# Latent attention on one Trainium2 core: scores with keys on partitions instead of queries, the row maximum folded into a matmul, and the division by the row sum moved behind the output matmul

## The chip, the core and the metric

The kernel runs on one core of a Trainium2 chip. TensorE (PE) multiplies matrices into PSUM; VectorE (DVE), ScalarE (ACT) and GpSimd (POOL) work on SBUF, the first two also on PSUM; SyncE (SP) issues the DMAs. The metric is the device time of one execution in microseconds. A few of the profile's names: PEld is the weight load of TensorE, PEclk the share of its full clock that was granted, and L123 is line 123 of the kernel.

## What is computed

Two layers run over 1024 latent tokens and 256 context tokens of width 1024. The first is a gated linear recurrence (HGRN2), the second multi-head latent attention. The change lies in the second layer alone, which is for 16 heads:

```python
def _attend(q_nope, q_pe, k_nope, k_pe, v):
    s = (jnp.einsum('bqhd,bkhd->bhqk', q_nope, k_nope, preferred_element_type=jnp.float32)
         + jnp.einsum('bqhr,bkr->bhqk', q_pe, k_pe, preferred_element_type=jnp.float32))
    p = jax.nn.softmax(s * MLA_SCALE, axis=-1)
    return jnp.einsum('bhqk,bkhd->bqhd', p.astype(v.dtype), v)
...
    def readout(o, z):
        B, L = o.shape[:2]
        return (o.reshape(B, L, D_INNER) * jax.nn.silu(z)) @ w_out
```

There are 1024 queries and 1280 keys a head. Keys and values of all heads come from one 128-wide latent and a 64-wide rotary part, so the kernel folds each head's key matrix into its queries and each head's value matrix into its output: all heads use the same `kh`, `kl`, `kr` and `vh`, `vl`.

## The kernel before

Everything is float32. To multiply at the rate of the faster float32r format without losing digits, a value is split into a rounded high part and a low part that holds the rest (`split`, L208: a ScalarE cast, then a VectorE subtraction), and a product is three matmuls: high by high, high by low, low by high (`mm3`, L263 to L265).

A tile is 128 tokens. Attention has 128 query tiles (8 for each of 16 heads), in 64 units of two. Per query tile `attn_scores` (L839) holds the queries still and streams the keys past them in blocks of 512, 512 and 256 columns, five matmuls a block (L855 to L859). A row of scores then lies in one partition: VectorE takes its extreme (L861, L867), ScalarE takes the exponential and the row sum (L871), VectorE divides the row by the sum (L877 to L882). Per unit `attn_values` (L885) transposes these probabilities on TensorE, 20 blocks of 128x128 (L902, tile `pt`), splits them (ScalarE `ph` L214, VectorE `pl` L215, both reading `pt` in PSUM), accumulates `pv` with 30 matmuls of 256 columns (L263 to L265), splits the result (`o32`, `oh` on ScalarE, `ol` on GpSimd, L920 to L922), multiplies by the head's value matrix (three matmuls), multiplies by the gate `za` on VectorE (L927, tile `ya`), and stores it to DRAM.

`attn_prep` (L783) makes the next head's operands in steps: two small float32 matmuls and the split of their result (`wqh`, `wql`), for every second head eight transposes of the rotary queries with their split (`qrh`, `qrl`, L818 to L826), and two blocks of 512 queries (six matmuls of 512 columns each, split into `wl`, `wh`). Each step goes through the PSUM tag `pt`, of which there are three buffers.

`attend` (L930) sorts all these steps by a time written out by hand. This order binds TensorE alone (`AT_ORDER`); a scheduler orders the other engines. Behind attention comes the output product of 16 heads; its first 8 heads for two token tiles (`lead`, L1197) are laid over the end of attention. SP's order is the scheduler's, before and after.

Of the kernel before, what the change touches and what calls it, by code (L numbers as in the profile page):

```python
# [9 lines left out]
F32 = mybir.dt.float32  # L10
# [27 lines left out]
class Net:  # L38
# [631 lines left out]
    def mla_in(self, pool, pp, kp, a, hh, hl, st):  # L670
# [6 lines left out]
        for c in range(NT):  # L677
# [39 lines left out]
            )  # L717
            if lat:
                j = c - NC
                nc.scalar.activation(junk, ps[:, 192:448], AF.Square, accum_out=ss[:, 1:2])  # L720
                r = self.rsq(pool, ss[:, 1:2], QR, 1)
                qn = t(pool, [P, QR], F32, "qn")
                nc.vector.tensor_scalar(qn, ps[:, 192:448], r, None, ALU.mult)
                q32 = t(pool, [P, 2, P], F32, "q32")
                for k in range(2):
                    nc.tensor.transpose(tp[:, (2 + k) * P : (3 + k) * P], qn[:, k * P : (k + 1) * P], self.ident)
                    nc.scalar.activation(q32[:, k], tp[:, (2 + k) * P : (3 + k) * P], AF.Copy, scale=qg[:, k : k + 1])
                js = slice(j * P, (j + 1) * P)
                self.split(st["qh"][:, :, js], st["ql"][:, :, js], q32)
# [53 lines left out]
    def attn_prep(self, pool, pp, a, st, qrD, zT, h, box):  # L783
# [23 lines left out]
        if h % 2 == 0:  # L807
# [6 lines left out]
            for b, n in self.qgs:  # L814
                sl = slice(b * P, (b + n) * P)
                ps = t(pp, [P, 512], F32, G_TAG)
                for j in range(n):
                    nc.tensor.transpose(ps[:, j * P : (j + 1) * P], qr[:, b + j], self.ident)  # L818
                for i, (rh, rl) in enumerate(box["pair"]):
                    own, twin = (slice(0, 64), slice(64, P))[:: 1 - 2 * i]  # L820
                    src = ps[own, : n * P]
                    nc.scalar.activation(rh[own, sl], src, AF.Copy, scale=SCALE)
# [16 lines left out]
    def attn_scores(self, pool, pp, st, box, i, prs):  # L839
        nc, t, NT = self.nc, self.t, self.NT  # L840
        mm = nc.tensor.matmul
        LK = NT * P
        blocks = [(o, min(512, LK - o)) for o in range(0, LK, 512)]
        nb = len(blocks)
        h, j = divmod(i, self.NL)
        qah, qal, rh, rl = box[h][:4]
        js = slice(j * P, (j + 1) * P)
        mx = t(pool, [P, 4], F32, "mx")
        sm = t(pool, [P, 4], F32, "sm")
        pr = t(pool, [P, LK], F32, "pr")  # L850
        sc = []
        for b, (o, w) in enumerate(blocks):
            s = t(pp, [P, 512], F32, "s")
            ks = slice(o, o + w)
            mm(s[:, :w], qah[:, js], st["kh"][:, ks], start=True, stop=False)  # L855
            mm(s[:, :w], qah[:, js], st["kl"][:, ks], start=False, stop=False)  # L856
            mm(s[:, :w], qal[:, js], st["kh"][:, ks], start=False, stop=False)  # L857
            mm(s[:, :w], rh[:, js], st["kr"][:, ks], start=False, stop=False)  # L858
            mm(s[:, :w], rl[:, js], st["kr"][:, ks], start=False, stop=True)  # L859
            with self.tc.high_priority(offset=AT_PRIO):  # L860
                nc.vector.tensor_reduce(mx[:, b : b + 1], s[:, :w], AX.X, ALU.min)  # L861
            sc.append(s)
            if b < nb - 1:
                yield
        nm = t(pool, [P, 1], F32, "nm")
        with self.tc.high_priority(offset=AT_PRIO):
            nc.vector.tensor_reduce(nm, mx[:, :nb], AX.X, ALU.min)  # L867
        for b, (o, w) in enumerate(blocks):
            yield
            with self.tc.high_priority(offset=EXP_PRIO):  # L870
                nc.scalar.activation(  # L871
                    pr[:, o : o + w], sc[b][:, :w], AF.Exp, bias=nm, scale=-1.0,
                    accum_out=sm[:, b : b + 1],
                )
        yield
        rs = t(pool, [P, 1], F32, "rs")
        nc.vector.tensor_reduce(rs, sm[:, :nb], AX.X, ALU.add)  # L877
        nc.vector.reciprocal(rs, rs)
        if i % NORM_ACT[1] < NORM_ACT[0]:
            nc.scalar.activation(pr, pr, AF.Copy, scale=rs)  # L880
        else:
            nc.vector.tensor_scalar(pr, pr, rs, None, ALU.mult)  # L882
        prs[i] = pr

    def attn_values(self, pool, pp, st, box, u, prs, yT):  # L885
        nc, t, NT = self.nc, self.t, self.NT
        tiles = [i for i in (2 * u, 2 * u + 1) if i < self.NH * self.NL]
        h, b = divmod(tiles[0], self.NL)
        n = len(tiles)
        N = n * P  # L890
        wvh, wvl, z = box[h][4:]
        np_ = -(-NT // 2)
        parts = {}
        acc = None
        for e in range(np_ + PV_LAG):
            if e < np_:
                m = min(2, NT - 2 * e)
                tp = t(pp, [P, 2, 2 * P], F32, "pt")
                for c in range(m):
                    for j, i in enumerate(tiles):  # L900
                        k = 2 * e + c
                        nc.tensor.transpose(  # L902
                            tp[:, c, j * P : (j + 1) * P], prs[i][:, k * P : (k + 1) * P], self.ident
                        )
                ph = t(pool, [P, 2, 2 * P], F32R, "ph")
                pl = t(pool, [P, 2, 2 * P], F32R, "pl")
                self.split(ph[:, :m, :N], pl[:, :m, :N], tp[:, :m, :N])
                parts[e] = (m, ph, pl)
            if e >= PV_LAG:
                if acc is None:  # L910
                    acc = self.pv[:, u % 2]
                m, ph, pl = parts.pop(e - PV_LAG)
                for c in range(m):
                    k = 2 * (e - PV_LAG) + c
                    self.mm3(acc[:, :N], st["vh"][:, k], st["vl"][:, k], ph[:, c, :N], pl[:, c, :N], k == 0, k == NT - 1)
            yield
        oh = t(pool, [P, 2 * P], F32R, "oh")
        ol = t(pool, [P, 2 * P], F32R, "ol")
        o32 = t(pool, [P, 2 * P], F32, "o32")
        nc.scalar.copy(o32[:, :N], acc[:, :N])  # L920
        nc.scalar.copy(oh[:, :N], o32[:, :N])
        nc.gpsimd.tensor_tensor(ol[:, :N], o32[:, :N], v32(oh[:, :N]), ALU.subtract)  # L922
        yield
        ps = t(pp, [P, 512], F32, G_TAG)
        self.mm3(ps[:, :N], wvh, wvl, oh[:, :N], ol[:, :N], True, True)
        y = t(pool, [P, 2 * P], F32, "ya")
        nc.vector.tensor_tensor(y[:, :N], ps[:, :N], z[:, b * P : b * P + N], ALU.mult)  # L927
        nc.sync.dma_start(yT[h][:, b * P : b * P + N], y[:, :N])

    def attend(self, pool, pp, a, st, qrD, zT, yT, box, tail):  # L930
        NL, NH = self.NL, self.NH
        n = NH * NL
        self.pv = self.t(pp, [P, 2, 2 * P], F32, "pv")
        prs = {}
        steps = []
        for h in range(1, NH):
            t0 = NL * (h - 1) + 3 + AT_LAG
            g = self.attn_prep(pool, pp, a, st, qrD, zT, h, box)
            gap = min(0.9, (NL - 4 - AT_LAG) / 5)
            steps += [(t0 + (e + (PREP_LATE if e > 1 and h % 2 == 0 else 0)) * gap, g) for e in range(6)]  # L940
        nb = -(-self.NT * P // 512)
        for i in range(n):
            g = self.attn_scores(pool, pp, st, box, i, prs)
            steps += [(i + b / nb, g) for b in range(nb)]
            steps += [(i + (nb - 1) / nb + EXP_AT[min(b, 2)], g) for b in range(nb)]
            steps += [(i + NORM_AT, g)]
        np_ = -(-self.NT // 2)
        for u in range(-(-n // 2)):
            g = self.attn_values(pool, pp, st, box, u, prs, yT)
            steps += [(2 * u + 2 + AT_LAG + e * 2 / np_, g) for e in range(np_ + PV_LAG + 2)]  # L950
        steps += [(n + TAIL_AT + TAIL_GAP * k, tail) for k in range(NH)]
        steps = sorted(enumerate(steps), key=lambda x: (x[1][0], x[0]))
        for _, (_, g) in steps:
            next(g, None)
# [24 lines left out]
def body(tc, a, out, dims):  # L979
    D, NH, NC, NL = dims  # L980
    NT = NC + NL
    with ExitStack() as ctx:
# [8 lines left out]
        zT = [t(dpool, [P, NL * P], F32, f"zT_{h}") for h in range(NH)]  # L991
        yT1 = [t(dpool, [P, NL * P], F32, f"yT1_{h}") for h in range(NH)]
# [113 lines left out]
        with ExitStack() as c3:  # L1106
# [55 lines left out]
            "kr": t(kpool, [P, NT * P], F32R, "kr"),  # L1162
            "qh": t(kpool, [P, 2, NL * P], F32R, "qh"),
            "ql": t(kpool, [P, 2, NL * P], F32R, "ql"),
        }
        with ExitStack() as c4:
# [30 lines left out]
        def lead():  # L1197
            head.extend(accs(sp, "s", 2))
            for k in range(K_LEAD if NH > K_LEAD else NH // 2):
                ld = net.op_load(mo, a["w_mo"], yT1, k, mg[0])  # L1200
# [4 lines left out]
        with ExitStack() as c5:  # L1205
            pool = Split(early, EARLY, Bufs(TP(c5, "at", 1), AT_BUFS))
            pp = Split(ep, EARLY, sp)
            with tc.manual_schedule(engines=AT_ORDER):
# [51 lines left out]
PREP_LATE = 0.5  # L1260
# [3 lines left out]
TAIL_AT = 0.2  # L1264
TAIL_GAP = 0.45
# [3 lines left out]
    "qr": 1, "wk": 2, "qrh0": 2, "qrl0": 2, "qrh1": 2, "qrl1": 2, "pr": 7, "ph": 4, "pl": 4,  # L1269
    "mx": 4, "sm": 4, "nm": 4, "rs": 4, "wvh": 2, "wvl": 2, "ya": 2, "oh": 2, "ol": 2,  # L1270
# [4 lines left out]
EARLY = {"wk", "qr", "za0", "wv32", "wvh", "wvl", "wqh", "wql", "qrh0", "qrl0", "pt", "pv"}  # L1275
AT_PSUM = {"s": 4, "pt": 3, "pv": 1}
G_TAG = "pt"
EXP_AT = (0.1, 0.25, 0.4)
NORM_ACT = (0, 2)
AT_PRIO = 60  # L1280
EXP_PRIO = 0
NORM_AT = 1.0
SCALE = -float((128 + ROPE) ** -0.5)
AT_ORDER = {mybir.EngineType.PE}
AT_LAG = 1.0
PV_LAG = 2
# [104 lines left out]
```

## Time and profile before

| | before |
|---|---|
| median of 3 runs | 3146.39 us (3146.16 to 3146.5) |
| the profiled execution's own time | 3146.84 us |
| its span, first to last instruction | 3145.1 us |
| mean granted TensorE clock | 0.995 |
| first and last score matmul | 2130.8 and 2949.2 us |
| last matmul into `pv` | 2983.0 us |
| busy in 2254 to 2306 us (one head) | PE 52.00, DVE 39.98, ACT 31.97, POOL 3.48 us |

The times in a timeline row are the start within the span and the duration, both in us. A matmul's duration holds its way through the array; the next one starts long before it ends, so the cost of a matmul in a stream is the distance between two starts. A group's row has busy time, then the mean duration in ns, then the idle time before it.

### The profile page before, as it was taken

Reading aid. Unit: us, or ns where it says so; the run is one execution under the profiler, and the core shown is the slowest. Engines: PE = TensorE matmul, PEld = TensorE weight load, DVE = VectorE, ACT = ScalarE, POOL = GpSimd, SP = SyncE. Lnnn points to the kernel's source line nnn. Section 1 sums busy time; section 2 is a strip of 40 time slices with the busy share of each in tenths; the row PEclk is TensorE's granted clock in tenths of the full one; section 3 lists DMA queues with packets and bytes.
Section 4 is the critical chain, followed back from the end, with each engine's and each line's share of the span. In section 5 each row is a group of like instructions: output and inputs, shape, how many; then the busy total and the mean of one; then the engine's idle time right before and its main releaser. Section 6 shows DMA issues by size and latency. Waiting matters only on the chain.

```text
span 3145.1 us, 51475 instructions
## 1 busy us (share of the span) xinstructions
PE 3108.3 (99%) x19412; PEld 2782.5 (88%) x19412; DVE 2164.4 (69%) x4898; ACT 1729.6 (55%) x4263; POOL 188.3 (6%) x305
## 2 busy tenths in 40 slices
PE   8899999999999999999999999999999999999999
PEld 7889989899898998988988888788999999999887
DVE  7777688776886758757585563536777777777642
ACT  6556465564655646655475563224666666666532
POOL 0000000000000000000000011000010000000000
PEclk8999999999999999999999999999999999999999
DMA  5110212102111021010127661430101011101261
GB/s 212 43 56 23 74 36 63 56 23 75 36 56 57 24 73 36 30 40 25 41 69 243 222 197 45 141 117 24 41 30 38 24 34 34 34 28 38 69 219 57
DMA packets 100009, 218.88 MB, mean 70 GB/s; under 512 B 10289, under 2 KB 47409, under 8 KB 99761
## 3 DMA queue, kind: packets, MB, share of 16 engines
q1 hardware_dynamic: 99760, 215.59, 21.1%
q8 instruction: 153, 2.51, 0.3%
q14 instruction: 96, 0.78, 0.1%
HBM read 175.70 MB, written 39.85 MB: 69 GB/s over the span
## 4 chain that ended last, share of the span: by engine, by line
PE 92%; DVE 3%; issue 2%; DMA 2%; ACT 1%; POOL 0%; SPq 0%; DVEq 0%; POOLq 0%; ACTq 0%
PE g L265 12%; PE g L264 12%; PE g L263 12%; PE lv L335 6%; PE pt L902 4%; PE o L486 3%; PE pv L263 2%; PE s L855 2%; PE pv L264 2%; PE pv L265 2%; PE s L856 2%; PE s L858 2%; PE s L859 2%; PE s L857 2%; PE lv L263 2%; PE lv L265 2%
## 5 line engine op out<-in xcount | busy, mean ns | idle before, releaser
L263 PE MATMUL g<-hh,wh 128*128 128x512 f32 (+1 forms) x1512 | 548.4, 363 | 3.3 <-DVE hh L253 1.6
L265 PE MATMUL g<-hl,wh 128*128 128x512 f32 (+1 forms) x1512 | 542.4, 360 | 3.0 <-DVE hl L254 3.0
L264 PE MATMUL g<-hh,wl 128*128 128x512 f32 (+1 forms) x1512 | 543.3, 359 | 0.0
L263 PEld LDWEIGHTS g<-hh,wh 128*128 128x128 f32 x1512 | 286.5, 189 | 40.6 <-DVE hh L253 2.0
L265 PEld LDWEIGHTS g<-hl,wh 128*128 128x128 f32 x1512 | 285.7, 189 | 39.0 <-DVE hl L254 3.8
L215 DVE TENSOR_TENSOR wl<-raw,wh 128x1024 fp32r<-128x1024 f32 (+1 forms) x170 | 207.7, 1224 | 160.8 <-ACT wh L214 149.4
L264 PEld LDWEIGHTS g<-hh,wl 128*128 128x128 f32 x1512 | 286.4, 189 | 35.9
L861 DVE TENSOR_REDUCE mx<-s 128x1 f32<-128x512 f32 (+1 forms) x384 | 229.7, 599 | 94.5 <-PE s L859 93.0
L871 ACT ACTIVATE pr<-s,nm 128x512 f32<-128x512 f32 (+1 forms) x384 | 232.7, 615 | 99.1 <-DVE nm L867 92.8
L335 PE MATMUL lv<-QX,KX 128*128 128x128 f32 x1920 | 263.1, 275 | 5.8 <-ACT QX L407 4.3
L335 PEld LDWEIGHTS lv<-QX,KX 128*128 128x128 f32 x1920 | 246.6, 192 | 14.8 <-ACT QX L407 5.5
L214 ACT CAST wh<-raw 128x1024 fp32r<-128x1024 f32 (+1 forms) x170 | 178.0, 1049 | 121.8 <-PE lv L264 38.2
L214 ACT CAST ph<-pt 128x512 fp32r<-128x512 f32 x320 | 187.8, 587 | 96.2 <-PE pt L902 86.6
L215 DVE TENSOR_TENSOR pl<-pt,ph 128x512 fp32r<-128x512 f32 x320 | 219.4, 686 | 12.6 <-ACT ph L214 12.5
L263 PE MATMUL g<-wh,hh 128*128 128x256 f32 (+2 forms) x676 | 197.6, 293 | 0.0
L263 PE MATMUL pv<-ph,vh 128*128 128x256 f32 x640 | 196.7, 307 | 0.0
L265 PE MATMUL g<-wl,hh 128*128 128x256 f32 (+2 forms) x676 | 196.4, 291 | 0.0
L902 PE MATMUL pt<-ident,pr 128*128 128x128 f32 x1280 | 192.5, 273 | 0.1
L264 PE MATMUL g<-wh,hl 128*128 128x256 f32 (+1 forms) x654 | 187.9, 287 | 0.0
L407 ACT COPY KX<-K 128x256 f32<-128x256 f32 (+1 forms) x288 | 109.6, 381 | 131.3 <-PE lv L335 71.3
L265 PE MATMUL pv<-pl,vh 128*128 128x256 f32 x640 | 180.2, 282 | 0.0
L264 PE MATMUL pv<-ph,vl 128*128 128x256 f32 x640 | 180.0, 281 | 0.0
(557 smaller groups left out, 7918.3 us busy)
## 6 DMA issues: line engine op xcount, KB each, us to landing
raw<-in_w_o SPq DMA_DIRECT2D x64, 512.0 KB, 3.8
raw<-in_w_qfbz SPq DMA_DIRECT2D x61, 512.0 KB, 3.8
raw<-in_ada_wT SPq DMA_DIRECT2D x32, 512.0 KB, 3.6
raw<-in_w_mo SPq DMA_DIRECT2D x24, 512.0 KB, 3.9
raw<-in_w_v SPq DMA_DIRECT2D x16, 512.0 KB, 3.6
yT<-Z SPq DMA_DIRECT2D x32, 256.0 KB, 2.0
raw<-in_w_z SPq DMA_DIRECT2D x16, 512.0 KB, 4.1
pyr<-yT SPq DMA_DIRECT2D x64, 128.0 KB, 3.7
```

The costliest lines, as they stand in the source:

```text
L214: nc.scalar.copy(hi, src)
L215: (eng or nc.vector).tensor_tensor(lo, src, v32(hi), ALU.subtract)
L263: mm(ps, lh, rh, start=first, stop=False)
L264: mm(ps, ll, rh, start=False, stop=False)
L265: mm(ps, lh, rl, start=False, stop=last)
L335: nc.tensor.matmul(ps[:, sl], lhs[:, sl], rhs[:, sl], start=True, stop=True)
L407: cp(m12(N[:]), m12(Y))
L486: nc.tensor.matmul(o[:, sl], l, r, start=i == 0, stop=i == len(ops) - 1)
L855: mm(s[:, :w], qah[:, js], st["kh"][:, ks], start=True, stop=False)
L861: nc.vector.tensor_reduce(mx[:, b : b + 1], s[:, :w], AX.X, ALU.min)
L871: nc.scalar.activation(pr[:, o : o + w], sc[b][:, :w], AF.Exp, bias=nm, scale=-1.0, accum_out=sm[:, b : b + 1],)
L902: nc.tensor.transpose(tp[:, c, j * P : (j + 1) * P], prs[i][:, k * P : (k + 1) * P], self.ident)
```

## The change

**Scores.** A unit of two query tiles now holds 128 keys still and streams 256 queries: ten key tiles, two to a PSUM bank, four matmuls each (L859), so that a column of `s` is a query and the probabilities come out with keys on partitions, as the second product wants them. The 20 transposes are gone.

**Maximum.** It must now be taken across partitions: VectorE takes it over the five banks elementwise (`m2`, L863 and L865) and over the last pair (`mf`, L873), TensorE transposes `mf` twice (L876), VectorE reduces (`mr`, L879), TensorE spreads the result over partitions (L882), ScalarE writes its negative into row 64 of the low rotary queries (L887). A fifth matmul of each key tile, `k5` by `rl` (L893), adds the low rotary part and the negative maximum to the scores still lying in PSUM; row 64 of `k5` is one. Only then comes the exponential (L896), without a bias and without the sum.

**Sum and division.** GpSimd adds the five probability tiles (four additions of 128x512, one of 128x256, L904 to L910). One unit after the values TensorE sums over partitions with a matmul by ones (L949), VectorE takes the reciprocal (L954), it goes to DRAM and comes back spread over partitions (L955, L960), and GpSimd multiplies `ya` by it (L962).

**Splits and buffers.** Probabilities are split out of SBUF, not PSUM. `ol` moves from GpSimd to VectorE (L945). PSUM has one buffer of `pt` instead of three; `mt` and `s5` take the other two.

**Order.** `attend` writes out one loop over units: scores of unit u, values of u-2, output of u-3, splits of u-1, a step of `attn_prep` behind the second and the fourth score bank. The order now binds TensorE, VectorE, ScalarE and GpSimd (`AT_HAND`). In the last five units `lead` also loads and splits the first four output weights.

```diff
+            nc.scalar.copy(st["k5"][:64, sl], tp[:64, P : 2 * P])
...
+                for i, (l, r) in enumerate(((kh, qah), (kl, qah), (kh, qal), (kr, rh))):
+                    mm(o, l[:, ks], r[:, js], start=c + i == 0, stop=c == m - 1 and i == 3)
...
+                    nc.vector.tensor_tensor(m2[:, :m], m2[:, :m], s[:, :m], ALU.max)
...
+            nc.tensor.transpose(mt[:, 0, j * P : (j + 1) * P], mf[:, j * P : (j + 1) * P], self.ident)
...
+            nc.vector.tensor_reduce(mr, mt[:, 0, :N].rearrange("p (j k) -> p j k", k=P), AX.X, ALU.max)
...
+            nc.scalar.activation(rl[64:65, js], mt[64:65, 1, :N], AF.Copy, scale=-1.0)
...
+                mm(s[:, c], st["k5"][:, ks], rl[:, js], start=False, stop=c == m - 1, skip_group_check=True)
...
+                nc.scalar.activation(p[:, :m], s[:, :m], AF.Exp)
...
+            add(l2, whole[0], whole[1], ALU.add)
+            for p in whole[2:]:
+                add(l2, l2, p, ALU.add)
...
-        nc.gpsimd.tensor_tensor(ol[:, :N], o32[:, :N], v32(oh[:, :N]), ALU.subtract)
...
+        nc.vector.tensor_tensor(ol, o32, v32(oh), ALU.subtract)
...
+        nc.vector.reciprocal(rc, ps[:, 2 * P : 2 * P + n])
+        nc.sync.dma_start(self.lD[u : u + 1, :N].rearrange("o (j p) -> p (o j)", p=P), rc)
...
+        nc.gpsimd.tensor_tensor(y, y, rb, ALU.mult)
...
+            for e in range(nb):
+                if e in (0, nb - 1) and rest:
+                    next(rest[0], None)
+                if cur:
+                    next(cur)
+                if nxt and low and e in PREP_AT:
+                    next(nxt, None)
+                if old and e == min(LOW_AT, nb - 1):
+                    next(old)
+                if e in SPLIT_AT:
+                    split(u - 1)
...
-            with tc.manual_schedule(engines=AT_ORDER):
+            with tc.manual_schedule(engines=AT_HAND):
...
-AT_PSUM = {"s": 4, "pt": 3, "pv": 1}
+AT_PSUM = {"pt": 1, "pv": 1, "mt": 1, "s5": 1}
...
+PREP_AT = (1, 3)
+SPLIT_AT = (4,)
+LOW_AT = 2
```

VectorE, in the middle of attention. Before, around the point where the next head's first step comes; `pl` reads the transposed probabilities `pt` in PSUM, `wvl` and `wql` belong to that step:

```order
L861 TENSOR_REDUCE mx_26038<-s_26041 128x1
L927 TENSOR_TENSOR ya_26056<-pt_26052,za_4730_24690 128x256
L212 SCALAR_TENSOR_TENSOR wql_26034<-pt_26030,wqh_26033 128x256
L877 TENSOR_REDUCE rs_26048<-sm_25938 128x1
L215 TENSOR_TENSOR wvl_26026<-wv_5048_26024,wvh_26025 128x128
L878 RECIPROCAL rs_26048<-rs_26048 128x1
L215 TENSOR_TENSOR pl_26065<-pt_26059,ph_26064 128x512
L882 TENSOR_SCALAR pr_25939<-pr_25939,rs_26048 128x1280
```

Now the same place in the new order, from the second score bank to the reduction of the maximum; `m` is `m2`, `p` and `ph` lie in SBUF:

```order
L863 TENSOR_TENSOR m_5056_26538<-m_5056_26538,s_26549 128x512
L215 TENSOR_TENSOR wvl_26567<-wv_5062_26565,wvh_26566 128x128
L212 SCALAR_TENSOR_TENSOR wql_26575<-pt_26571,wqh_26574 128x256
L863 TENSOR_TENSOR m_5056_26538<-m_5056_26538,s_26578 128x512
L945 TENSOR_TENSOR ol_26532<-o_5054_26533,oh_26531 128x256
L863 TENSOR_TENSOR m_5056_26538<-m_5056_26538,s_26589 128x512
L826 SCALAR_TENSOR_TENSOR qrl_4032_21668<-pt_26601,qrh_5070_26599 64x512
L826 SCALAR_TENSOR_TENSOR qrl_4033_21669<-pt_26601,qrh_5071_26600 64x512
L863 TENSOR_TENSOR m_5056_26538<-m_5056_26538,s_5073_26614 128x512
L873 TENSOR_TENSOR mf_26625<-m_5056_26538 128x256
L215 TENSOR_TENSOR pl_26628<-p_26506,ph_26627 128x512
L215 TENSOR_TENSOR pl_26632<-p_26510,ph_26631 128x512
```

The steps of the next head stand between the maxima of this unit's score banks, and the splits behind them read two operands in SBUF.

GpSimd, in the middle of attention. Before, `ol` is one instruction a unit, and `qrh` copies come for every second head:

```order
L922 TENSOR_TENSOR ol_25166<-o_4845_25167,oh_25165 128x256
L922 TENSOR_TENSOR ol_25320<-o_4881_25321,oh_25319 128x256
L826 COPY qrh_4905_25404<-qrh_4905_25404 64x512
L826 COPY qrh_4906_25405<-qrh_4906_25405 64x512
L922 TENSOR_TENSOR ol_25517<-o_4930_25518,oh_25516 128x256
```

Now one unit and the start of the next; the first `l` names are the 128x512 accumulator `l2`, `rb` is the spread reciprocal:

```order
L904 TENSOR_TENSOR l_5311_27738<-p_27719,p_27723 128x512
L906 TENSOR_TENSOR l_5311_27738<-l_5311_27738,p_27727 128x512
L906 TENSOR_TENSOR l_5311_27738<-l_5311_27738,p_27731 128x512
L906 TENSOR_TENSOR l_5311_27738<-l_5311_27738,p_27735 128x512
L910 TENSOR_TENSOR l_27737<-l_5311_27738 128x256
L962 TENSOR_TENSOR ya_27706<-ya_27706,rb_27749 128x256
L904 TENSOR_TENSOR l_5344_27897<-p_27878,p_27882 128x512
```

GpSimd has six two-operand instructions a unit where it had one, in a chain that begins with the unit's second probability tile.

## What the change is forecast to do

> **What bounds the kernel now.** I read the page first, then the busy times of single heads inside attention, then TensorE's waits there.
>
> ```profile
> span 3145.1 us, 51475 instructions
> PE 3108.3 (99%) x19412; PEld 2782.5 (88%) x19412; DVE 2164.4 (69%) x4898; ACT 1729.6 (55%) x4263; POOL 188.3 (6%) x305
> 2254.00:2306.00 52.00, 52.00 (x358) 47.68 (x357) 39.98 (x87) 31.97 (x84) 3.48 (x5) 1.00 0.10 29
> PE s L855 <- ACT pr L871: 2.9, 2, 2.4
> ```
>
> The third row is one head: TensorE is busy for all 52.00 us, VectorE for 39.98, ScalarE for 31.97, GpSimd for 3.48, at the full clock (1.00). The last row is TensorE's whole waiting between 2150 and 2950 us: 2.9 us. So attention costs what TensorE's stream costs, and a busy TensorE says nothing of peak; the distances between starts do.
>
> ```profile
> 2499.85 0.60 PE L902 MATMUL pt<-ident,pr 128*128 128x128 f32 x4
> 2500.21 0.37 PE L263 MATMUL pv<-ph,vh 128*128 128x256 f32 x1
> 2500.41 0.28 PE L264 MATMUL pv<-ph,vl 128*128 128x256 f32 x1
> 2500.54 0.28 PE L265 MATMUL pv<-pl,vh 128*128 128x256 f32 x1
> 2501.01 0.40 PE L855 MATMUL s<-kh,wl 128*128 128x512 f32 x1
> 2502.18 0.28 PE L263 MATMUL pt<-oh,wvh 128*128 128x256 f32 x1
> ...
> 2215.41 1.02 POOL L922 TENSOR_TENSOR ol<-o,oh 128x256 fp32r<-128x256 f32 x1 [4.58 <-issue]
> 2230.53 0.73 POOL L922 TENSOR_TENSOR ol<-o,oh 128x256 fp32r<-128x256 f32 x1 [11.82 <-PE s L859]
> 2242.42 0.74 POOL L922 TENSOR_TENSOR ol<-o,oh 128x256 fp32r<-128x256 f32 x1 [11.16 <-ACT oh L921]
> 2318.63 1.02 POOL L922 TENSOR_TENSOR ol<-o,oh 128x256 fp32r<-128x256 f32 x1 [4.58 <-issue]
> ```
>
> Four transposes take 0.36 us until the next matmul, and that one stands 0.20 ahead of its successor where 0.12 is usual: 0.11 us a transpose. From 2500.54 to 2501.01 run four matmuls of 256 columns: 0.118 each. From 2501.01 to 2502.18 run five of 512: 0.234 each. A unit of two query tiles is 20 x 0.11 + 20 x 0.234 + (10 + 30 + 3) x 0.118 = 2.2 + 4.68 + 5.07 = 11.95 us. The `ol` rows, one a unit, agree: 2230.53 to 2242.42 is 11.89. From 2215.41 to 2318.63 are eight units with the preparation of two heads: 12.90 us a unit, so a head's preparation costs 51.6 - 4 x 11.9 = about 4 us of TensorE.
>
> **What the change takes from and adds to TensorE.** Gone: the 20 transposes, 2.2 us. The scores are 40 + 10 matmuls of 256 columns, 5.90 us, where they were 4.68 + 1.18 = 5.86. New small ones: two transposes of `mf`, two spreads of `mr`, two sums by ones. The trace has no spread and no one-column matmul in a stream; as transposes they are 6 x 0.11 = 0.66, and the ends are 0.06 (no charge but the next one's weight load) and 0.20 (the row at 2500.21) each, so 0.36 to 1.2 us. I take 0.66, since all six are 128 wide or load 128 columns. Values and output keep 33 x 0.118. The new unit is 83 x 0.118 + 0.66 = 10.45 us, 1.50 us less; over 64 units **-96 us**, with -61 and -115 at the ends.
>
> **What must keep up.** The other engines' new work, from the nearest rows:
>
> ```profile
> L365 DVE TENSOR_TENSOR UL<-U,UH 128x512 fp32r<-128x512 f32 x16 | 11.1, 694 | 0.0
> L779 DVE TENSOR_TENSOR zst<-zst,lv 128x512 f32<-128x512 f32 x32 | 21.9, 686 | 62.3 <-ACT zst L778 62.1
> L254 DVE TENSOR_TENSOR hl<-h,hh 128x256 fp32r<-128x256 f32 x16 | 6.3, 422 | 15.4 <-ACT hh L253 15.4
> L823 DVE SCALAR_TENSOR_TENSOR qrl<-pt,qrh 64x512 fp32r<-64x512 f32 x32 | 21.8, 685 | 0.9
> L871 ACT ACTIVATE pr<-s,nm 128x512 f32<-128x512 f32 x256 | 173.9, 685 | 99.1 <-DVE nm L867 92.8
> L364 ACT CAST UH<-U 128x512 fp32r<-128x512 f32 x16 | 9.9, 621 | 3.5 <-DVE U L361 3.5
> L920 ACT COPY o<-pv 128x256 f32<-128x256 f32 x64 | 23.8, 372 | 72.1 <-PE pv L265 72.1
> L921 ACT CAST oh<-o 128x256 fp32r<-128x256 f32 x64 | 26.1, 407 | 2.0
> L639 POOL TENSOR_TENSOR pss<-pss x18: 192/318/1233, 1699.7 to 3139.4; 128x1 f32<-128x1 f32 x18
> L922 POOL TENSOR_TENSOR ol<-o,oh x64: 730/737/1078, 2162.2 to 2984.5; 128x256 fp32r<-128x256 f32 x64
> ```
>
> VectorE, a unit: five maxima (one operand in PSUM, 686), five splits (both in SBUF, 694), `mf`, `ol`, the reduction and `ya` (about 420 each), a reciprocal: 8.7 us, and since successive instructions start some 0.08 us before the last one ends, 7.5; with a quarter of a head's preparation (3.2 us: two `qrl`, two query splits of that size, two small ones) 8.3 us. ScalarE: 5 x 0.685 + 5 x 0.621 + 0.372 + 0.407 + 0.4 for row 64 = 7.7 us. GpSimd: no row has an addition of 512; 192 ns for one element and 737 for 256 give 2.14 ns an element, so 1.285 us (737 and 1474 are the ends); 4 x 1.285 + 2 x 0.737 = 6.6 us. Each is under 10.45: none is the bound by its work alone. What decides is who waits for whom.
>
> **VectorE and GpSimd share something.** The splits read PSUM before; now both operands lie in SBUF, while GpSimd has 6.6 us of work there.
>
> ```profile
> 674.38 1.22 DVE L365 TENSOR_TENSOR UL<-U,UH 128x1024 fp32r<-128x1024 f32 x1
> ...
> 674.67 0.99 POOL L81 TENSOR_SCALAR rsq_m<-oss 128x4 f32<-128x4 f32 x1 [81.00 <-ACT ojunk L490]
> 678.64 0.19 POOL L81 TENSOR_SCALAR rsq_m<-oss 128x4 f32<-128x4 f32 x1 [1.84 <-ACT ojunk L490]
> ...
> 591.75 1.14 POOL L81 TENSOR_SCALAR rsq_m<-oss 128x2 f32<-128x2 f32 x1 [4.61 <-ACT ojunk L490]
> 592.98 0.70 POOL L82 TENSOR_TENSOR rsq_m<-rsq_m,nhalf 128x2 f32<-128x2 f32 x1
> ...
> 591.52 0.65 DVE L406 TENSOR_TENSOR QX<-QX,T 128x256 f32<-128x256 f32 x1
> 592.07 0.44 DVE L406 TENSOR_TENSOR KX<-KX,Ta 128x256 f32<-128x256 f32 x1
> ...
> 593.40 0.66 DVE L408 TENSOR_TENSOR QY<-QX,T 128x256 f32<-128x256 f32 x1
> ...
> 678.32 0.43 DVE L408 TENSOR_TENSOR QY<-QX,Ta 128x256 f32<-128x256 f32 x1 [0.89 <-ACT QX L407]
> ```
>
> The same small GpSimd instruction takes 0.19 us, but 0.99 when it starts inside a VectorE subtraction of two SBUF operands, and it ends with that one (675.60). The other way, a VectorE product that starts 0.28 us before a GpSimd instruction ends takes 0.66 where a like one takes 0.43. So each waits until the other has finished. The Trainium skill (SBUF — State Buffer, "Who interferes with whom") says it as a rule: a VectorE instruction with two SBUF inputs and a GpSimd instruction that reads SBUF exclude each other for their whole length; these rows agree.
>
> Laid out on TensorE's clock, with 0 at a unit's first score matmul: the exponentials of the unit before run to 2.3 (they start some 0.75 before 0 and follow at 0.6), so GpSimd adds from about 0.6. Score banks come every 8 x 0.118 = 0.94 us, the last at 4.7. `ol` is ready for VectorE at 3.6 and waits for an addition until 4.6; the last two maxima end at 6.2, `mf` waits until 6.3 and ends at 6.7. TensorE has three of the five value steps in between (3 x 0.71) and wants `mf` at 6.84: in time by 0.1. Two splits and the reduction end at 8.3, TensorE wants `mr` at 8.3; the fifth value step covers row 64. So a plain unit has no slack and hardly a loss; I charge 0.2 us (0 to 1 for the ends) in the 27 units without a preparation step: **+5 us**.
>
> **The preparation through one `pt`.** Its first step now sits behind the second bank, its second use of `pt` behind the fourth, at 4.0 us, and needs `wql`.
>
> ```profile
> L796 ACT ACTIVATE wv<-wk,vec 128x128 f32<-128x128 f32 x16 | 6.4, 403 | 15.4 <-DMA wk<-in_w_abs 11.8 <-DVE wvl L215 3.5
> L211 ACT ACTIVATE wqh<-pt 128x256 fp32r<-128x256 f32 x16 | 6.1, 382 | 0.6 <-PE pt L800 0.6
> L214 ACT CAST wvh<-wv 128x128 fp32r<-128x128 f32 x16 | 5.0, 310 | 0.1
> ```
>
> ScalarE has its exponentials to 2.3, `o32` and `oh` to 3.1, then `wv`, `wvh`, `wqh` to 4.2; on VectorE `wvl` waits for an addition until 4.6, `wql` ends at 5.2. TensorE stands 1.2 us, with the maxima queued behind `wvl`. The later steps wait likewise for the splits of the step before: by the same count 0.8 and 0.3 us for heads with rotary transposes, 0.3 for the others. That is 2.3 and 1.5 us a head, 1.95 on average; 15 heads give **+29 us** (0 if ScalarE gets there earlier, 45 if each wait also hits a full addition).
>
> **With one answer.**
>
> ```profile
> pyr<-yT SPq DMA_DIRECT2D x64, 128.0 KB, 3.7
> ...
> L215 DVE TENSOR_TENSOR wl<-raw,wh 128x1024 fp32r<-128x1024 f32 (+1 forms) x170 | 207.7, 1224 | 160.8 <-ACT wh L214 149.4
> ```
>
> The reciprocal's way through DRAM is two transfers; `pyr<-yT` lands after 3.7 us, so some 7 us, and the product that waits has 10 us until GpSimd needs it; uncovered it would stop GpSimd, not TensorE. In SP's queue the loads of the next head stand ahead of those waits by several units. Ten copies into `k5` and a memset go beside a stage where ScalarE has room. Four early weight splits (1.22 us each on VectorE) lie in five units with 2 us of room there; uncovered 5 us. The first two units have no values to hide the maximum's round trip, about 2.5 us each, where the trace before has two of its waits too: **+2 us**.
>
> Sum against the profiled execution: 3146.84 - 96 + 5 + 29 + 2 = 3087; the median of the runs lies 0.45 under that execution, so **3086 us**.
>
> **Rivals.**
> 1. *Everything is absorbed.* ScalarE and VectorE run ahead, the preparation costs TensorE no stall: 3146.4 - 96 + 2 = 3052 us. For it: VectorE has 2 us of room a unit. Against: the order is now fixed on all four engines, so a late step cannot be passed.
> 2. *The shared access binds.* GpSimd's 6.6 us, six gaps of 0.09 (592.98 follows 0.09 behind its predecessor's end) and VectorE's two-operand work, 5 x 0.694 + 2 x 0.422 = 4.3, make 11.45 us, more than TensorE's 10.45. The 27 plain units then cost 11.45: 27 x 0.8 more than forecast, 3108 us. For it: every term has a row. Against: the probability tiles let GpSimd lag by most of a unit into the longer units. It is what the rule of the Trainium skill (SBUF — State Buffer, "Who interferes with whom") would make of a unit.
> 3. *VectorE becomes the bound, slower than before.* Its queue is in order; if `ol`, `mf`, the first and the third split each meet a fresh addition, it stands 4 x 1.285 = 5.1 us a unit: 8.3 + 5.1 = 13.4 against 12.9 now, 64 x 0.5 = 32 us more, 3179 us. It decides from 4.6 us of waiting a unit. Against: the layout above has two such entries at under 1 us, and VectorE keeps the access through instructions that follow one another: the GpSimd step at 591.75 takes 1.14 us while two products and more go by.
>
> **Chances.** Forecast 0.45 (by itself 3068 to 3104), rival 1 0.22, rival 2 0.22, rival 3 0.08; 0.03 that gains and losses cancel. The range takes in the first three and the doubt on the small matmuls: 3046 to 3126. Faster by over 0.2% 0.89, within it 0.03, slower 0.08; 0.2% (6 us) is about what a measurement here can tell from no change.
>
> **What would show it.** In the profile after: `ya` products one plain unit apart by 10.5 to 10.7 us; TensorE's waits inside attention near 35 us, most of them before `pt` and on VectorE's `wql` and `qrl`; GpSimd's additions near 1.3 us, longer where a split runs; VectorE's `mf` and `ol` longer than 0.42. It is wrong if plain units take 11 us or more, if the waits before `pt` are missing, or if TensorE waits chiefly for `mf` or `mr`.

## The result and the profile after

The changed kernel takes 3285.69 us (median of 4 runs, 3282.96 to 3292.16) where the kernel before takes 3146.27, measured beside it (4 runs): a ratio of 1.0448 (95% interval 1.043 to 1.0466). The forecast was 3086 us, 60 us less than before; the time rose by 139 us. The profiled execution took 3285.55 us.

The page of the changed kernel, its busy times in 200 us of attention (the columns are PE, PEld, DVE, ACT, POOL, the granted clock, DMA share and GB/s), and TensorE's waits from 2130 to 3140 us:

```profile
span 3283.8 us, 53075 instructions
PE 3108.0 (95%) x19924; PEld 2817.2 (86%) x19924; DVE 2250.0 (69%) x4582; ACT 1672.6 (51%) x3889; POOL 603.8 (18%) x625
2400.00:2600.00 200.00, 177.92 (x1341) 170.71 (x1340) 157.90 (x231) 98.74 (x206) 105.54 (x92) 0.94 0.30 39
PE mt L882 <- DVE mr L879: 66.4, 47, 3.5
PE s L263 <- ACT pyh L214: 33.4, 6, 16.0
PE mt L876 <- DVE mf L873: 27.0, 34, 2.9
PE pt L263 <- DVE qrl L826: 6.6, 7, 0.9
```

TensorE is no longer full in attention, and its clock there is 0.94, where the same 200 us of the kernel before have 1.00. The stall before `pt`, on which the forecast spent 29 us, is 6.6 us; the waits are for the two steps of the maximum, which the prediction named as the sign that it is wrong. Read from the score matmuls (L859; L855 before) and the last matmul into `pv`:

| us | first score | first to last score | last score to end | span |
|---|---|---|---|---|
| before | 2130.8 | 818.4 | 195.9 | 3145.1 |
| after | 2139.7 | 894.8 | 249.2 | 3283.8 |
| difference | +9.0 | +76.4 | +53.3 | +138.7 |

From the third unit to the last, forty score matmuls follow forty every 14.2 us on average; the units of the runs below are averaged over the same stretch. The first four units, which have no product with 1/sum yet, took 11.3, 12.2, 11.6 and 11.0 us.

What the waits look like in one unit: GpSimd, then VectorE, then TensorE, the start, the duration and, in brackets, the idle time and who ended it.

```profile
2618.28 0.75 POOL L962 TENSOR_TENSOR ya<-ya,rb 128x256 f32<-128x256 f32 x1 [6.44 <-DVE m L863]
2618.98 1.48 POOL L904 TENSOR_TENSOR l<-p,p 128x512 f32<-128x512 f32 x1
2620.54 4.39 POOL L906 TENSOR_TENSOR l<-l,p 128x512 f32<-128x512 f32 x3
...
2620.74 1.38 DVE L873 TENSOR_TENSOR mf<-m 128x256 f32<-128x256 f32 x1
2622.04 3.44 DVE L215 TENSOR_TENSOR pl<-p,ph 128x512 fp32r<-128x512 f32 x2
2625.41 0.41 DVE L879 TENSOR_REDUCE mr<-mt 128x2 fp32r<-128x256 f32 x1
...
2625.87 0.44 PE L882 MATMUL mt<-identr,mr 128*128 128x128 f32 x2 [1.77 <-DVE mr L879]
```

GpSimd stands 6.44 us before the product. (The name in the bracket is inferred from what ended just then; what the product needs is the row `rb`, whose load was issued at 2613.18 us and takes 4.8 us at the median.) So its additions start in the middle of the unit and run through VectorE's folding maximum (1.38 us for 0.42) and the two splits behind it (3.44 for 1.29). The reduction `mr` stands behind those splits, and TensorE waits 1.77 us for it. It is a tidy story (VectorE and GpSimd take turns, the reduction is late), and my first theory, A. Theory B has the maximum's own way that long, without GpSimd. The experiments show that it tells how the delay travels and not where it comes from.

### The profile page after: what moved, and what is told of

Same layout as the page of the kernel before. It is cut to its first block, busy times and chain, and to the rows that moved or that the text cites. A ratio compares the mean times of both kernels' runs of the same rounds, so it can differ in the third digit from the quotient of the medians.

```text
span 3283.8 us, 53075 instructions
## 1 busy us (share of the span) xinstructions
PE 3108.0 (95%) x19924; PEld 2817.2 (86%) x19924; DVE 2250.0 (69%) x4582; ACT 1672.6 (51%) x3889; POOL 603.8 (18%) x625
## 5 line engine op out<-in xcount | busy, mean ns | idle before, releaser
L215 DVE TENSOR_TENSOR pl<-p,ph 128x512 fp32r<-128x512 f32 x320 | 315.4, 1032 | 2.8 <-ACT ph L214 2.7
L81 POOL TENSOR_SCALAR rsq_m<-oss 128x4 f32<-128x4 f32 (+1 forms) x48 | 26.4, 549 | 1529.4 <-ACT ojunk L490 1529.4
L906 POOL TENSOR_TENSOR l<-l,p 128x512 f32<-128x512 f32 x192 | 264.5, 1378 | 15.1
L214 ACT CAST ph<-p 128x512 fp32r<-128x512 f32 x320 | 177.0, 619 | 42.6 <-PE pv L264 42.4
L863 DVE TENSOR_TENSOR m<-m,s 128x512 f32<-128x512 f32 x256 | 175.0, 684 | 31.4 <-PE s L859 26.7
L896 ACT ACTIVATE p<-s 128x512 f32<-128x512 f32 x320 | 163.6, 608 | 57.0 <-PE s L893 57.0
L859 PE MATMUL s<-wl,kh 128*128 128x256 f32 x640 | 189.5, 296 | 0.9 <-ACT p L896 0.9
```

Source lines behind the costliest of these rows:

```text
L81: nc.gpsimd.tensor_scalar(m, ss, 1.0 / n, EPS, ALU.mult, ALU.add)
L214: nc.scalar.copy(hi, src)
L215: (eng or nc.vector).tensor_tensor(lo, src, v32(hi), ALU.subtract)
L859: mm(o, l[:, ks], r[:, js], start=c + i == 0, stop=c == m - 1 and i == 3)
L863: nc.vector.tensor_tensor(m2[:, :m], m2[:, :m], s[:, :m], ALU.max)
L896: nc.scalar.activation(p[:, :m], s[:, :m], AF.Exp)
```

## Experiments

Each is an edit of the changed kernel (3285.69 us).

**E1, no additions.** `l2` is the last probability pair; the four additions of 512 are left out, so the sum under the fraction holds the last pair of key tiles only.

```diff
-            add(l2, whole[0], whole[1], ALU.add)
-            for p in whole[2:]:
-                add(l2, l2, p, ALU.add)
+            l2 = whole[-1]
```

> GpSimd's four 128x512 additions of each unit are left out, so that the sum under the fraction holds the last pair of key tiles only (the output is not the attention's). Theory A (access: VectorE's folding maximum, splits and low part wait for whole additions of GpSimd, the reduction `mr` stands behind them and TensorE waits for it): the folding maximum falls from 1.01 us to 0.42-0.5 and the split from 1.03 to 0.69-0.75, TensorE's waits for `mf` and `mr` (93 us in all) fall under 15 us, the plain unit goes from 13.1-13.7 us to 11-11.7, and the kernel to 3130-3180 us. Theory B (the maximum's own way is that long, GpSimd has no part in it): the waits for `mf` and `mr` stay at 80 us or more and the kernel at 3270-3290 us.

3290.52 us (3287.4 to 3292.41). A falls, and B too, for the waits did change. TensorE's waits and SP's queue in E1:

```profile
PE s L859 <- ACT p L896: 80.2, 40, 4.4
...
PE mt L882 <- DVE mr L879: 24.8, 3, 21.9
PE mt L876 <- DVE mf L873: 8.4, 8, 2.4
...
2600.14 0.43 SPq L952 DMA_DIRECT2D lD<-rc  x1
2608.45 0.32 SPq L957 DMA_DIRECT2D rb<-lD  x1
2613.72 0.32 SPq L960 DMA_DIRECT2D yT<-ya  x1
2614.14 0.39 SPq L952 DMA_DIRECT2D lD<-rc  x1
```

TensorE waits as long as before, 113 us for 93 in these three rows and those of the changed kernel, but now mostly for probabilities (their buffers are held by the one addition that is left, behind the product) and once, in the last unit, 21.9 us for `mr`. Units still take 14.20 us on average. Something else sets 14.2 us, and the waits only show which engine happens to carry it.

**E4, all five splits behind the reduction.** `SPLIT_AT = ()` and no split between the two loops.

> All five splits of a unit stand behind the reduction `mr` on VectorE (in the changed kernel two stand between the folding maximum and it). Theory A with the order as its second half (the reduction is late because splits that wait for GpSimd stand ahead of it): TensorE's wait for `mr` falls from 66 us to under 15, the folding maximum still meets its addition (wait for `mf` stays at 20-40 us), units lose about 1 us and the clock's half-rate windows become fewer: 3200-3250 us. Theory B: the reduction is no earlier, 3270-3290 us. A new wait is possible: the third product of the values comes before its split, which would give some of it back (waits for `pl` then stand in place of `mr`).

3294.63 us (3291.79 to 3300.13). The reduction is on time and nothing is won: 1.3 us of waits for `mr` are left, 40.6 stand before `mf`, and the preparation's matmuls wait some 50 us for `pt`. Units take 14.23 us.

**E2, the product behind the next unit's additions.** In `attend`, the second step of `rest` moves from the fourth score bank to the end of the unit.

```diff
-                if e in (0, nb - 1) and rest:
+                if e == 0 and rest:
...
             for _ in cur or ():
                 pass
+            if rest:
+                next(rest[0], None)
```

> The product with 1/sum is issued to GpSimd behind the next unit's additions in place of ahead of them; the arithmetic is the same. Theory C (the additions collide because the product at the head of GpSimd's queue waits some 11 us for the row `rb` and starts them late, in the time of the folding maximum and the splits): the additions begin within 2 us of a unit's start, the folding maximum falls under 0.7 us, waits for `mf` and `mr` halve, and the kernel falls by 40 to 80 us, to 3205-3245 us. Theory A alone (some VectorE instruction of two SBUF operands meets an addition wherever the five additions lie): the collisions move to other instructions and the kernel stays within 20 us, 3265-3290 us.

3165.14 us (3159.36 to 3167.64): 120 us less, where theory C (the product starts the additions late) gave it 40 to 80: 12.38 us a unit, and 783.3 us from first to last score, 35 less than before the change. The edit moves two things, though: GpSimd's product, and with it the store of the product in SP's queue. SP, in the changed kernel and in E2, with SP's waits from 2300 to 2900 us (total, times, longest):

```profile
2605.61 0.43 SPq L955 DMA_DIRECT2D lD<-rc  x1
2613.18 0.32 SPq L960 DMA_DIRECT2D rb<-lD  x1
2619.06 0.32 SPq L963 DMA_DIRECT2D yT<-ya  x1
2619.47 0.39 SPq L955 DMA_DIRECT2D lD<-rc  x1
...
SPq L960 <- DMA lD<-rc: 323.0, 42, 8.9
SPq L963 <- POOL ya L962: 213.0, 42, 6.1
SPq L955 <- DVE m L863: 1.8, 5, 0.5
SPq L955 <- DVE wh L215: 1.1, 3, 0.4
```

```profile
2609.66 0.37 SPq L955 DMA_DIRECT2D lD<-rc  x1
2616.91 0.32 SPq L960 DMA_DIRECT2D rb<-lD  x1
2618.11 0.32 SPq L963 DMA_DIRECT2D yT<-ya  x1
2622.08 0.37 SPq L955 DMA_DIRECT2D lD<-rc  x1
...
SPq L955 <- DVE ya L957: 131.7, 47, 4.9
```

In the changed kernel SP is a ring of its own: write 1/sum, stand until it has landed (323.0 / 42 = 7.7 us), load the row, stand until GpSimd has multiplied with it (213.0 / 42 = 5.1 us), store the product, and only then write the next unit's 1/sum. With some 1.4 us for the issues and what lies between them that is 14.2 us, one unit. It hardly ever waits for VectorE before a write (1.8 + 1.1 us, in 8 of 42 units): the write of 1/sum is nearly always overdue. In E2 the store no longer waits for the row loaded just ahead of it, and SP waits 131.7 us for VectorE before its writes: the compute engines set the pace again. That leaves two theories. S: the ring in SP's queue is what costs the time. G: it is GpSimd's order, the product ahead of the additions.

**E3, no way through DRAM.** TensorE spreads 1/sum by a product with the identity, VectorE multiplies.

```diff
-        nc.sync.dma_start(self.lD[u : u + 1, :N].rearrange("o (j p) -> p (o j)", p=P), rc)
...
+            c = rc[:, j : j + 1].broadcast_to([P, P])
+            nc.tensor.matmul(rb[:, j * P : (j + 1) * P], c, self.ident, start=True, stop=True)
+        nc.vector.tensor_tensor(y, y, rb[:, :N], ALU.mult)
```

> 1/sum doesn't go through DRAM: TensorE spreads it over the partitions with a fp32 product with the identity (2 matmuls of 128 columns in four passes, an estimate of 0.5 us a unit from the 0.163 us of two transposes), VectorE multiplies from PSUM (0.42 us a unit), GpSimd has the additions alone. Theory C (round trip): the additions start early, as in e2, 40 to 80 us less between the scores, and the stretch from the last score to the end goes from 249 us to about 205 since SP's queue no longer stands for the two landings: 3170-3220 us. Theory A alone: the stretch of the scores stays within 20 us (the product's 0.5 us on TensorE may add up to 32 us), only the end falls: 3230-3290 us.

3144.24 us (10 runs, 3139.96 to 3147.18), ratio to the kernel before 0.9991 (0.9982 to 1.0001). Units take 12.40 us with 0.36 us of new matmuls in them, and the end 218.9 us for 249.2: both parts go with the way through DRAM (with it GpSimd's product is gone too).

**E5, ScalarE issues the write.** One word is changed, to open the ring in SP's queue and leave GpSimd's order alone: `nc.scalar.dma_start(self.lD[...], rc)`.

> One word of the changed kernel: ScalarE issues the write of 1/sum to DRAM in place of SyncE. GpSimd's order stays (the product ahead of the additions), SyncE's too but for the write that is gone. Theory S (ring in SyncE's queue: write of 1/sum 8.1 us, load of the row 4.8, product 0.7, store of the product, and only then the next unit's write, since it is queued behind the store: 14.2 us a unit whatever the other engines do): the next write no longer stands behind the product, the ring opens, the stretch from first to last score falls from 895 us to 770-800 and the kernel to 3155-3190 us. Theory G (it was GpSimd's order, which the product behind the additions mended: additions late, VectorE waits for them): GpSimd's order is untouched, the kernel stays at 3240-3290 us.

3279.64 us (3266.65 to 3286.48). Taken by its expectation this speaks for G, but the trace shows a new wait of my own making. ScalarE's and TensorE's waits, and ScalarE:

```profile
ACT qrl L887 <- DVE ya L957: 270.3, 61, 7.5
...
PE s L893 <- ACT qrl L887: 85.7, 63, 4.2
...
2616.93 0.37 ACTq L955 DMA_DIRECT2D lD<-rc  x1
2617.34 0.38 ACT L887 ACTIVATE qrl<-mt 1x256 fp32r<-1x256 f32 x1 [4.35 <-DVE ya L957]
```

The write waits in ScalarE's queue for a reciprocal that stands behind three splits on VectorE (the rows name `ya`, the instruction after it), and the copy of the negative maximum waits behind the write: TensorE stands 85.7 us for it, 1.4 us a unit, where the waits for `mr` are down to 9.7. So E5 decides nothing; E9 mends it.

**E6, the write as one row.** TensorE lays the sums in one partition (`matmul(ps[:1, 2P:2P+N], ones, l)`), the reciprocal is taken there, and the write is one row of 1 KB. All queues keep their order.

> All queues and their order stay as in the changed kernel; only the write of 1/sum is another: TensorE lays the sums in one row (ones as the 128x1 stationary, the partial sums as 256 moving columns), and the write is one row of 1 KB in place of 256 single elements. Theory S: the ring's first part falls from 8.1 us to about the 1.7-2.5 us of the other stores, the ring to 8-9 us, under TensorE's own 12.4 us a unit: 3140-3175 us. If the write's landing does not depend on its form, the ring stays 14 us and the kernel 3280-3290. Theory G: GpSimd's additions come earlier with the row too, so it would also gain here, by the waits it explains (up to 95 us).

3153.67 us (10 runs, 3150.54 to 3156.98), in the range of theory S: 132 us less with the same ring, shortened. SP and VectorE in E6:

```profile
2618.80 0.24 SPq L952 DMA_DIRECT2D lD<-l  x1
2619.90 0.33 SPq L957 DMA_DIRECT2D rb<-lD  x1
2625.89 0.32 SPq L960 DMA_DIRECT2D yT<-ya  x1
2631.45 0.24 SPq L952 DMA_DIRECT2D lD<-l  x1
...
L951 DVE RECIPROCAL l<-pt 1x256 f32<-1x256 f32 x48 | 83.4, 1738 | 0.0
```

The write is over within 1.1 us, the ring takes 7.1 us from write to store and then stands 5.6 us until the next reciprocal. GpSimd's order is untouched, its product still goes ahead of the additions. With the row there early, though, the product no longer holds the additions up, so a part of the 132 us can be G's; E9 asks how much the ring alone is worth.

**E9, ScalarE issues the write behind the copy of the negative maximum.**

> As the kernel in which ScalarE issues the write of 1/sum, but one place later: behind the copy of the negative maximum, so that TensorE no longer waits for that copy (86 us of waits with the write ahead of it). The write is still single elements (8 us), GpSimd's order still that of the changed kernel. Theory S (the ring closes in SyncE's queue, through the store ahead of the next write): with the ring open and that wait gone the units come to those of the kernel with the row, 12.55 us on average, and the kernel to 3150-3190 us. Theory G (GpSimd's order, product ahead of the additions): 3240-3290 us. Theory M (the ring closes through memory: the next write waits until the row has been read): 8 and 4.8 us still follow one another, units of 13 us or more, 3200-3250 us.

3206.4 us (3205.18 to 3207.78): the ring opened without a word changed on GpSimd is worth 79 us, in the range that I had given theory M. But M falls by the trace: the row of one unit is loaded from 2613.49 on and is there at 2618.84, when the product starts; the next write is issued at 2618.23, ahead of that, where M has it wait. What is left against E6 is 53 us. Some 27 of them lie between the scores (13.00 us a unit for 12.55) and are G's part by these rows:

```profile
PE s L859 <- ACT p L896: 30.0, 54, 3.0
...
2613.49 0.32 SPq L961 DMA_DIRECT2D rb<-lD  x1
...
2618.23 0.37 ACTq L958 DMA_DIRECT2D lD<-rc  x1
...
2618.84 0.72 POOL L963 TENSOR_TENSOR ya<-ya,rb 128x256 f32<-128x256 f32 x1 [4.46 <-DMA rb<-lD]
```

The product still stops GpSimd 4.5 us for the slow row, and the next unit's probability buffers come free late: 30.0 us of waits for them, 0.5 us a unit. Another 24 us lie behind the last score (241.2 us for 217.4), where the slow write and the load still follow one another.

**E7, the sums on all partitions.** `ones` becomes 128x128, so that one matmul gives every partition the sums; VectorE takes the reciprocal of 128x256 and multiplies. No DRAM, no product on GpSimd. **E8** is E7 without the four additions.

> No way through DRAM and no GpSimd product: the stationary of the sums' matmul is 128x128 ones, so that the sums arrive on all partitions (256 columns in four passes, an estimate of 0.45 us from four times 0.112), VectorE takes the reciprocal and multiplies (two instructions of 0.42 us if like the folding maximum undisturbed). Theory S: as the kernel with the spread by a product with the identity (3144 us) less that product's 0.36 us a unit: 3110-3135 us, and after the last values no wait of 16-17 us for the last head's load. Rival V (VectorE's extra 0.84 us a unit come ahead of the maximum and TensorE waits for it): 3140-3170 us.

> The kernel with the sums on all partitions, and GpSimd's four 128x512 additions of each unit left out (the sum holds the last pair of key tiles only; the output is not the attention's). It prices the meeting of VectorE and GpSimd once the ring is gone. Theory A in what is left of it: the folding maximum and the splits get shorter, TensorE's waits for them (about 10 us in the kernels without the ring) and a part of the preparation's waits go: 10-30 us faster than the kernel with the sums on all partitions. Theory S alone: VectorE and GpSimd have room, within 8 us of it.

E7 3143.08 us (10 runs; ratio to before 0.9988, 0.9978 to 0.9997), E8 3114.06 (ratio 0.9891, 0.9876 to 0.9905). E7 missed its range: its plain units, those without a step of the preparation, take as long as E3's, 11.07 us. VectorE has a reciprocal of 1.75 us more to do, and in the unit shown by E7's trace at 2434.80 us TensorE starts the transposes of `mf` 0.24 us late; in the like unit of E8, with the same reciprocal and no additions, it does not. VectorE's groups between 2300 and 2900 us, E7 first, then E8:

```profile
L951 DVE RECIPROCAL rc<-pt 128x256 f32<-128x256 f32 x49 | 85.8, 1751 | 0.0
...
L945 DVE TENSOR_TENSOR ol<-o,oh 128x256 fp32r<-128x256 f32 x49 | 34.4, 703 | 0.0
...
L873 DVE TENSOR_TENSOR mf<-m 128x256 f32<-128x256 f32 x48 | 27.7, 577 | 1.7
...
L954 DVE TENSOR_TENSOR ya<-ya,rc 128x256 f32<-128x256 f32 x49 | 41.5, 847 | 1.7
```

```profile
L873 DVE TENSOR_TENSOR mf<-m 128x256 f32<-128x256 f32 x51 | 21.7, 425 | 1.8
...
L942 DVE TENSOR_TENSOR ol<-o,oh 128x256 fp32r<-128x256 f32 x51 | 21.4, 419 | 0.0
...
L951 DVE TENSOR_TENSOR ya<-ya,rc 128x256 f32<-128x256 f32 x50 | 21.3, 425 | 1.7
```

With the ring gone, the additions cost 29 us, 0.45 us a unit; beside them `ol`, `mf` and the product take 0.28, 0.15 and 0.42 us longer on average.

**E10 and E11, two banks for the preparation.** E7 and E3, with the preparation's steps in the bank of `mt` and in `pt` by turns, head 0's also in that of `s5`.

```diff
+        tags = iter((G_TAG, "mt", "s5") * 4) if h == 0 else iter(("mt", G_TAG) * 4)
...
-        ps = t(pp, [P, 512], F32, G_TAG)
+        ps = t(pp, [P, 512], F32, next(tags))
```

> The kernel with the sums on all partitions (3143 us), and a head's preparation takes the bank of the transposed maximum (free in the first half of a unit) and `pt` in turn, head 0's also the bank of the last score pair. It prices the prediction's term for the single `pt`. If preparation's gaps of 0.5 to 1.2 us before its matmuls (two or three a head) are waits for `pt`: 1.5-2.5 us a head and some 4-9 us at the start go, 3100-3125 us. If VectorE is late there anyway (its reciprocal of 128x256 takes 1.75 us): within 10 us of 3143.

> The same turn of banks in the kernel with 1/sum spread by TensorE (3144 us), which has VectorE's time and pays 0.36 us a unit on TensorE instead. Waits for `pt`: 3100-3125 us; otherwise within 10 us of 3144. It should be below the kernel before (3147 us) by more than 0.5% in the first case.

3129.85 us (5 runs, 3129.69 to 3130.97) and 3129.51 (5 runs, 3127.25 to 3130.62). E11 against E3 is 14.7 us and E10 against E7 13.2 us, the price of one `pt` with head 0's share in it (the kernel before took 1.8 and 0.5 us longer beside the later runs, so it may be 2 us more). Both gained less than forecast; why is not shown: TensorE still waits 9.9 us for `mf` in E11, but it did so for 8.9 us in E3. E11 is 0.9937 of the kernel before (0.9925 to 0.995): with E10, level with it, the fastest version with the reference's arithmetic, and 0.6% faster than the kernel before.

## Why the prediction was wrong

**The step that failed** is the one under "With one answer": "the product that waits has 10 us until GpSimd needs it; uncovered it would stop GpSimd, not TensorE", at no cost. I asked who needs the row, and not what the queue that brings it does next. Three things were missed there. The trip's length: "some 7 us" from a load that lands in 3.7, where the write of single elements takes 8.1 us (median) and the load behind it 4.8. Its recurrence: the store waits for the product, the next write stands behind the store, so trips can't overlap and one unit can't be shorter than one trip. And its place at the end, where the last head's output can't be loaded before its trips are done. There, SP's and TensorE's rows of the changed kernel; the loads of the last heads' outputs (`pyr`) stand behind both trips:

```profile
3106.35 0.42 SPq L955 DMA_DIRECT2D lD<-rc  x1
...
3118.41 0.32 SPq L960 DMA_DIRECT2D rb<-lD  x1
...
3119.30 0.38 SPq L594 DMA_DIRECT2D pyr<-yT  x1
...
3124.11 2.08 PE L263 MATMUL s<-wh,pyh 128*128 128x512 f32 x4 [16.04 <-ACT pyh L214]
```

Between the scores the slow trip costs 894.8 - 794.2 = 100.6 us by E6, which shortens it and touches no order, and 111.5 by E2, which also takes the product out of the additions' way. Opening the ring alone, as E9 does, gives 894.8 - 821.7 = 73.1.

**SP's queue** I looked at only for loads of the next head "ahead of those waits by several units". That the same queue holds three steps of one dependent chain stands in the order of the changed kernel, without a run.

**TensorE's stream** was right in kind and 0.26 us a unit too short. In E2, with the waits aside, the spacings are 0.118 us for scores and values; the six small matmuls come to 0.36 (sums) + 0.14 + 0.17 = 0.67 us, 0.66 forecast. That they agree is luck: the sums cost more than forecast, the other four less, and the forecast's 0.11 for each was to hold the delay of the matmul behind it. That delay comes on top: the matmul behind each of the three small groups, and the first of a unit, is 0.17 to 0.20 us ahead of its successor in place of 0.118 (2606.84 to 2607.04 us in E2). So the stream of a unit is some 10.7 us, not 10.45 (E2 from 2609.35 to 2621.45 us, 12.10 less 1.39 for six matmuls of the preparation): 17 us over 64 units. E7 and E8 have plain units of 11.07 and 10.75 us.

**VectorE and GpSimd.** The exclusion is there, but the step "VectorE keeps the access through instructions that follow one another" did not hold: in the unit shown `mf` and each of the two splits let one addition pass, 3.44 us for two splits. The Trainium skill (SBUF — State Buffer, "Who interferes with whom") has it that "Issue order, not op shape, decides who blocks". The rows of that unit agree; the prediction's row at 591.75 us does not, where VectorE's instructions at 592.07 us and after went ahead of a GpSimd step that was already there. What decides between two that wait stays open. The term was 5 us; E7 less E8 gives 29. Rival 3 named the instructions that would meet an addition, and rival 3's price, 3179, was too small because it took these meetings for the cause: E1 takes them away and nothing comes back. Its sign, slower, came true for another reason.

**The single `pt`** was put at 29 us between the scores and is 9 to 11 there (785.0 - 776.1 in E3 and E11, 781.4 - 770.7 in E7 and E10), 13 to 15 in all.

**The sum.** The forecast's span has 756.4 us between the scores. The ring and the product's place add 111.5, and E2's 783.3 leaves 27: the additions are 24 more than forecast, TensorE's stream 17 more, the single `pt` 18 to 20 less, and some 5 stay open. At the end 53 us came on top: E3, E6 and E7 give back 29 to 32 of it, so these go with the slow trip. Of the rest, 12 to 14 are the drain, in which the values are two units behind the scores (last score to last matmul into `pv`: 34 us before, 63 in the changed kernel, 46 to 48 in E3, E6 and E7); some 9 behind it stay open. I had 2 us for both ends. The start cost 9 us in the profiled execution; what in it does, and what the banks give back, is not shown, for E10's first score comes 6.6 us earlier than E7's and E11's only 1.2 earlier than E3's. What the clock's fall to 0.94 adds by itself stays open: in E2 the same window has 1.00 (the row below), but with its writes overdue SP's ring would, by this account, have filled any time that a full clock saved.

```profile
2400.00:2600.00 200.00, 192.27 (x1558) 186.04 (x1557) 156.56 (x266) 115.74 (x241) 115.15 (x106) 1.00 0.32 43
```

## What to carry to other kernels

When a value takes a trip through DRAM, write down all that its queue issues in one round, in order, and sum the landings that it waits for: that sum is a lower bound for the loop, whatever the engines have to do. In a trace the sign is a queue whose round starts late and never waits for what it is to write (SP waited some 3 us in 42 units ahead of its writes of 1/sum, and 536 us inside the round), while the waits on the compute engines only show where the delay surfaces, and removing the one that is named moves it to the next.

## What the hardware showed unasked

- A write of 256 single elements of 4 bytes to DRAM takes 6.6 to 12.0 us to land (median 8.1, 57 landings in the changed kernel); the same kilobyte as one row is there within 1.1 us of its issue (E6).
- VectorE's reciprocal of 256 columns takes 1751 ns (E7), and 1738 ns in one partition (E6); of two columns, 0.16 us (the changed kernel). 1751 ns is 6.8 ns a column and four times the 425 ns of a product of that shape (E8). The Trainium skill (VectorE: DVE Perf Modes, "First, the fixed hardware budget") says that the divider iterates with a repeat count of 8. That agrees in kind; no run here shows the count.
